# A chunked RWKV-7 recurrence in two groups of four pairs of heads, with a narrower state that VectorE decays

## The chip, the cores and the metric

The kernel runs on one core of a Trainium2 chip. The core has TensorE (PE; its weight loads are shown as PEld), VectorE (DVE), ScalarE (ACT), GpSimd (POOL), SyncE (SP, which issues most DMAs here) and 16 DMA engines. The metric is the device time of one execution of the whole program in microseconds; the median of the runs shown is compared.

## What is computed

A decoder trunk of two layers over 1024 tokens of width 1024 in float32. Layer 0 mixes tokens with a gated MLP, layer 1 with RWKV-7; each is followed by cross-attention into 256 memory rows and a SwiGLU feed-forward. The change lies in RWKV-7's recurrence. It has 16 heads of 64 channels, each with a state of 64 by 64:

```python
def step(S, inp):
    r_t, w_t, k_t, v_t, a_t, b_t = inp
    sa = jnp.einsum('bhij,bhj->bhi', S, a_t)
    S = S * w_t[:, :, None, :] + sa[..., None] * b_t[:, :, None, :] + v_t[..., None] * k_t[:, :, None, :]
    return S, jnp.einsum('bhij,bhj->bhi', S, r_t)
```

Here `a = -kk`, `b = kk * ah`, and `w` is a decay in (0, 1). The output y is normalised by head, gets a bonus term, is multiplied by a gate and projected by `w_o`.

## The kernel before, in words

The 1024 tokens are cut into 16 chunks of 64, and inside a chunk the recurrence is written as matrix products. Four chunks are a batch (256 tokens), so there are four batches, b = 0 to 3. The 16 heads are eight pairs p of two heads (128 channels, which fill the partitions); two pairs that are prepared together are an index pi = 0 to 3.

For each batch the stages are:

- `rwkv_prep(b, pi)` loads the decay's logarithm, keys and so on from DRAM (SP's queue), scans the decay inside each chunk (L1265), takes exponentials, and makes for two pairs: AR (a and r times the decay since the chunk's start), BK (b and k divided by it), the masked products GA and GR of BK with AR (L1300, L1303), BT (BK transposed on TensorE, L1307, copied by ScalarE, L1308), UV (v, and GA times v, L1324) and D, the decay over a whole chunk, one number for each channel (L1272). AR, GR, BT and UV lie in the pool `A`, which has 32 buffers for everything in the kernel; BK and GA take the pool `bk`, which has four.
- `rwkv_solve(b)` inverts the triangular 32 by 32 blocks of GA for all heads and chunks at once: 31 rows in order on VectorE (L1348, L1345) with GpSimd (L1352). Its input and its result go through DRAM (D1 and D4, D2 and D3).
- `rwkv_merge(b)` puts the 32-blocks together into Z, the inverse of the 64 by 64 blocks (32 by 32 products on TensorE, L1386 and L1395).
- `rwkv_chunks(b)` is the recurrence: 4 chunks times 8 pairs, 32 steps.
- `rwkv_post(b, pi)` normalises y, adds the bonus, multiplies by the gate and writes z to DRAM.

A step of the recurrence (`one`) for a chunk and a pair goes from engine to engine. The state `s0` of a pair is a 128 by 128 tile, of which only the two diagonal blocks of 64 by 64 are meaningful in the end; one full product with AR gives both the solve's right side and the old state's share of y (L1422). VectorE adds UV (L1423, into `rs`). Two products with Z give u, one for each head, which ScalarE copies into UV (L1429). Then follow a product of the identity with the state (it puts the old state into PSUM), two products of GR with UV for y, and two of BT with UV which add to the state in PSUM. ScalarE copies y over AR (L1438) and copies the state back, times D (L1441). All of these products but the first go through the helper `mm`, so the profile shows them under L1409, and they are told apart by the tiles that they read. A float32 product with a stationary operand is shown as two instructions.

Each step takes one PSUM bank of the pool `ck`, which has four. `order` sets the order in which the program writes the steps (chunk by chunk, pair by pair), with the parts of neighbouring steps woven together. The functions are generators; `stagger` runs several of them in turn, `run` exhausts one, `later` puts one into a queue of tasks, and `tick` and `drain` advance that queue. The scheduler that places the instructions on each engine takes the order in which they are written as a priority and sets up the semaphores.

In `rwkv` the loop over b = 1 to 3 writes the steps of batch b-1, the solve of b, puts the post stage of b-1 into the queue, and writes prep of b+1 and merge of b. For b = 3 it stops after the steps of batch 2 and the solve. The output projection of the first 512 tokens follows; between its two halves (`between`) come the merge and the steps of batch 3.

Of the kernel before, what the change touches and what calls it, by code (L numbers as in the profile page):

```python
# [12 lines left out]
P = 128  # L13
S = 1024
D = 1024
# [6 lines left out]
class Trunk:  # L22
# [1227 lines left out]
    def rwkv_prep(self, R, B, pi, b, d, C):  # L1250
# [43 lines left out]
        for q in range(2):  # L1294
            qs = slice(q * 4, q * 4 + 4)
            for h in range(2):
# [7 lines left out]
                yield  # L1304
            ps = self.bank()
# [95 lines left out]
    def rwkv_chunks(self, R, B, b, states):  # L1401

        nc = self.nc
        heads = [slice(h * 64, h * 64 + 64) for h in range(2)]
        if b == 0:
            for p in range(KD):
                states[p] = R['st'].tile([P, P], F32, name='s', tag=f's{p}')
                nc.gpsimd.memset(states[p], 0.0)
        mm = lambda o, l, r: nc.tensor.matmul(o, lhsT=l, rhs=r, start=False, stop=True, skip_group_check=True)  # L1409

        def one(c4, p):
            pi, c = (p // 2, p % 2 * 4 + c4)
            T = B['T'][pi]
            AR, UV, BT, GR = (T['AR'], T['UV'], T['BT'], T['GR'])
            zr, to = (heads[pi % 2], heads[c % 2])
            bk = self.bank_ck()
            ar, u, sp = (bk[:, 0:128], bk[0:64, 128:256], bk[:, 256:384])
            s0 = states[p]
            last = b == 3 and c4 == 3
            rs = R['rs'][pi % 2][(p // 4 * 2 + p % 2) % 4]  # L1420
            uvc = UV[0:64, c].rearrange('i h v -> i (h v)')
            nc.tensor.matmul(ar, lhsT=AR[:, c, :, :], rhs=s0, start=True, stop=True)  # L1422
            nc.vector.tensor_add(rs[zr, :], ar[0:64, :], uvc)  # L1423
            if not last and False:
                nc.scalar.activation(s0, s0, AF.Copy, scale=T['D'][:, c:c + 1])
            yield
            for h, hs in enumerate(heads):
                mm(u[:, hs], R['Z'][pi // 2][:, h, c, :], rs[:, hs])
            nc.scalar.copy(uvc, u)  # L1429
# [8 lines left out]
            e = lambda: nc.scalar.copy(AR[to, c - c % 2].rearrange('i a v -> i (a v)'), ar[64:128, :])  # L1438
            e()
            if not last:  # L1440
                nc.scalar.activation(s0, sp, AF.Copy, scale=T['D'][:, c:c + 1])  # L1441
            if not 1:
                e()
        order = sorted(((c4, p) for c4 in range(4) for p in range(KD)), key=lambda x: x[0] * 8 + x[1] + 1 * (x[1] // 2))
        if not 1:
            for c4, p in order:
                for _ in one(c4, p):
                    pass
                yield
            return  # L1450
        live = []
        for c4, p in order:
# [56 lines left out]
    def rwkv(self, W, C, filler, mk_close):  # L1509
# [24 lines left out]
        def prep(b):  # L1534
            return stagger([self.rwkv_prep(R, B[b], pi, b, D_[0], C) for pi in range(4)], 7 if b else 6)

        def chunks(b):
            yield from self.rwkv_chunks(R, B[b], b, states)

        def post(b):  # L1540
# [164 lines left out]
```

## Time and profile before

| | us |
|---|---|
| median of 3 runs | 3295.14 (3293.02 to 3295.4) |
| the profiled execution | 3312.53 |
| its span, first to last instruction | 3310.8 |

The profile is of one execution. Its page gives the busy time of each engine; the other views that are used below are a table by stretches of time (busy time of each engine, the number of instructions, then PEclk, the TensorE clock granted as a share of full speed, the busy share of the DMA engines, and GB/s), a timeline of instructions (start, duration, engine, line, operation, out<-in tiles, shape, count of instructions merged into the row), groups of instructions by line and shape (count, then busy time, mean duration in ns, and the idle time of the engine just before them with what ended it), and the list of waits (who waited for whom: total, times, longest). Matrix products overlap in the pipeline, so their cost is read from the distance between starts and not from their durations. A shape such as `128*64 128x64` is a stationary operand of 128 partitions by 64 columns, and an output of 64 columns.

The mean granted clock of the whole span is 0.956.

### The profile page before, as it was taken

The page shows a single profiled execution, that of the slowest core. Times are in us where ns is not written, and L with a number is a line of the kernel's source. Part 1 is how long each engine was busy: PE and PEld are TensorE (multiplying, and loading weights), DVE is VectorE, ACT ScalarE, POOL GpSimd, SP SyncE. Part 2 cuts the span into 40 slices and gives each one's busy share as a digit, 9 for nine tenths or more (in the row PEclk, how much of TensorE's full clock was granted, in tenths as well). Part 3 has the DMA queues.
Part 4 walks back from the last instruction along what each step waited for, and adds up shares of the span by engine and source line. Part 5 has one row for each costly group of instructions (what it writes and reads, how often), then busy time and mean ns, then how long its engine had stood idle before and what let it go on. Part 6 is the DMA issues. An engine that isn't in the chain of part 4 may idle for free. (4 is left out here: it accounts for less than half of the span.)

```text
span 3310.8 us, 44442 instructions
## 1 busy us (share of the span) xinstructions
PE 3135.4 (95%) x16570; PEld 2545.7 (77%) x16570; DVE 2025.2 (61%) x2876; ACT 1490.8 (45%) x2759; POOL 1058.4 (32%) x800
## 2 busy tenths in 40 slices
PE   8999999899999888999889899999999899999897
PEld 6888888778888666888667787887788688887676
DVE  5463545655444998755766567545545744445998
ACT  5443544533333433766743454445545533334332
POOL 0000011443334654311512244223011533334664
PEclk9999999999999999999999888779999999999998
DMA  5622544332222432744956644335554233323322
GB/s 186 204 77 70 197 147 141 114 96 83 77 77 85 144 102 77 238 136 131 301 173 169 169 121 100 105 92 176 178 163 150 65 96 86 86 77 120 103 96 96
DMA packets 448407, 421.97 MB, mean 127 GB/s; under 512 B 76672, under 2 KB 351264, under 8 KB 448192
## 3 DMA queue, kind: packets, MB, share of 16 engines
q1 hardware_dynamic: 441280, 393.96, 38.8%
q0 software_dynamic: 6912, 25.17, 2.4%
q8 instruction: 131, 2.15, 0.3%
q14 instruction: 84, 0.69, 0.1%
HBM read 314.13 MB, written 104.92 MB: 127 GB/s over the span
## 5 line engine op out<-in xcount | busy, mean ns | idle before, releaser
L438 PE MATMUL ps<-a,wh 128*128 128x512 f32 x2464 | 772.6, 399 | 6.1 <-DVE a L119 4.6
L119 DVE TENSOR_TENSOR wl<-wr,wh 128x1024 fp32r<-128x1024 f32 (+1 forms) x369 | 447.6, 1223 | 349.8 <-ACT wh L118 349.2
L438 PEld LDWEIGHTS ps<-a,wh 128*128 128x128 f32 x2464 | 465.6, 189 | 123.2 <-DVE a L119 7.0
L118 ACT CAST wh<-wr 128x1024 fp32r<-128x1024 f32 (+1 forms) x369 | 323.5, 889 | 522.4 <-PE ps L438 180.1
L438 PE MATMUL ps<-a,wl 128*128 128x512 f32 x1232 | 479.6, 397 | 0.0
L606 PE MATMUL ps<-wh,a 128*128 128x512 f32 x1136 | 380.3, 408 | 48.6 <-DVE a L615 32.6
L148 PE MATMUL ps<-a,wh 128*128 128x512 f32 (+1 forms) x848 | 330.3, 395 | 10.9 <-ACT a L118 5.9
L149 PE MATMUL ps<-a,wh 128*128 128x512 f32 (+1 forms) x848 | 325.7, 386 | 2.2 <-DVE a L119 2.2
L150 PE MATMUL ps<-a,wl 128*128 128x512 f32 (+1 forms) x848 | 325.4, 386 | 1.6 <-DVE wl L119 1.5
L148 PE MATMUL ps<-wh,a 128*128 128x512 f32 x800 | 313.9, 402 | 13.7 <-DVE a L1504 4.8
L149 PE MATMUL ps<-wl,a 128*128 128x512 f32 x800 | 318.5, 398 | 0.6 <-DVE wl L119 0.6
L150 PE MATMUL ps<-wh,a 128*128 128x512 f32 x800 | 316.7, 400 | 0.0
L606 PEld LDWEIGHTS ps<-wh,a 128*128 128x128 f32 x1136 | 218.9, 193 | 120.7 <-DVE a L615 32.5
L438 PEld LDWEIGHTS ps<-a,wl 128*128 128x128 f32 x1232 | 233.2, 189 | 57.6 <-DVE wl L119 0.8
L119 DVE TENSOR_TENSOR wl<-s,wh 128x512 fp32r<-128x512 f32 (+1 forms) x200 | 210.8, 1066 | 76.6 <-ACT wh L118 73.7
L118 ACT CAST wh<-s 128x512 fp32r<-128x512 f32 (+1 forms) x200 | 129.8, 662 | 251.0 <-PE ps L438 91.8
L606 PE MATMUL ps<-wl,a 128*128 128x512 f32 x568 | 228.8, 403 | 0.0
L208 POOL TENSOR_TENSOR sm<-sm,mhalf 128x4 f32<-128x4 f32 (+3 forms) x60 | 67.5, 1127 | 498.1 <-DVE sm L228 422.4
L119 DVE TENSOR_TENSOR a<-a 128x1024 fp32r<-128x1024 f32 (+1 forms) x134 | 208.1, 1567 | 24.3 <-ACT a L118 22.3
L615 DVE TENSOR_TENSOR a<-ps,a 128x512 f32<-128x512 f32 x304 | 194.8, 676 | 13.5 <-PE ps L606 13.4
L148 PEld LDWEIGHTS ps<-a,wh 128*128 128x128 f32 x848 | 163.3, 194 | 43.8 <-ACT a L118 6.8
L148 PEld LDWEIGHTS ps<-wh,a 128*128 128x128 f32 x800 | 151.9, 190 | 51.4 <-DVE a L1504 5.3
(273 smaller groups left out, 5631.7 us busy)
## 6 DMA issues: line engine op xcount, KB each, us to landing
wr<-in_ffn_w_in SPq DMA_DIRECT2D x90, 512.0 KB
scr<-t SPq DMA_DIRECT2D x136, 256.0 KB
scr<-t SPq DMA_DIRECT2D x60, 512.0 KB
a<-scr SPq DMA_DIRECT2D x108, 256.0 KB
wr<-in_rw_w_rkv SPq DMA_DIRECT2D x48, 512.0 KB
t<-scr SPq DMA_DIRECT2D x36, 512.0 KB
ld<-scr SPq DMA_DIRECT2D x72, 256.0 KB
wr<-in_xa_wkv SPq DMA_DIRECT2D x32, 512.0 KB
```

The costliest lines, as they stand in the source:

```text
L118: self.nc.scalar.copy(hi, src)
L119: (engine or self.nc.vector).tensor_sub(lo, src, hi)
L148: nc.tensor.matmul(out, lhsT=ah, rhs=bh, start=start, stop=False)
L149: nc.tensor.matmul(out, lhsT=ah, rhs=bl, start=False, stop=False)
L150: nc.tensor.matmul(out, lhsT=al, rhs=bh, start=False, stop=stop)
L208: self.nc.gpsimd.tensor_tensor(out=r, in0=v, in1=self.mhalf[:, 0:n], op=ALU.pow)
L438: self.nc.tensor.matmul(out, lhsT=a, rhs=b, start=start and k == 0 and (i == 0), stop=k == 3 and i == 2, skip_group_check=True)
L606: nc.tensor.matmul(ps, lhsT=a, rhs=b, start=start and k == 0 and (q == 0), stop=k == K - 1 and q == 2, skip_group_check=True)
L615: nc.vector.tensor_add(o, ps, o)
```

## The change

The eight pairs become two groups of four pairs (pi 0 and 1; pi 2 and 3), and a step now serves one chunk of one pi, that is of two pairs: 16 steps in a batch. The state of a pi is a tile of 128 by 2 by 64: for each of its two pairs the two heads lie one under the other on the partitions, with 64 columns each. The first product is made per head, with 64 partitions of AR and of the state, and each head writes its own PSUM bank, so a step takes two banks of `ck`. The additions, the products with Z, GR and BT stay per head and pair; u of both pairs is copied at once. The product with the identity is gone: VectorE now decays the state and adds the product with BT in one instruction for each pair, reading the state from SBUF and the product from PSUM. Since D multiplied the product with BT too, prep now multiplies BK by D on GpSimd, ahead of the transposes that make BT and behind the products that use BK undecayed.

The order changes as well: the steps of group 0 of batch b-1 are woven with prep of batch b for group 1, and the steps of group 1 with the solve of b, with post of group 0 and with prep of batch b+1 for group 0. The steps of batch 3 are written with both groups in turn, and `between` drains the queue ahead of the merge.

In the diff, of the removed code only what runs is shown (the order was chosen by a constant, `o = 3`).

```diff
@@ rwkv_prep
+            nc.gpsimd.tensor_mul(BK[:, qs], BK[:, qs], T['D'][:, qs].rearrange('p (c a t) -> p c a t', a=1, t=1).broadcast_to([P, 4, 2, 64]))
             ps = self.bank()
             for c in range(4):
                 nc.tensor.transpose(ps[:, c * P:(c + 1) * P], BK[:, q * 4 + c, :, :], self.ident)
@@ rwkv_chunks
-    def rwkv_chunks(self, R, B, b, states):
+    def rwkv_chunks(self, R, B, b, states, group):
...
+        pis = range(2 * group, 2 * group + 2)
         if b == 0:
-            for p in range(KD):
-                states[p] = R['st'].tile([P, P], F32, name='s', tag=f's{p}')
+            for pi in pis:
+                states[pi] = R['st'].tile([P, 2, 64], F32, name='s', tag=f's{pi}')
...
-            nc.tensor.matmul(ar, lhsT=AR[:, c, :, :], rhs=s0, start=True, stop=True)
-            nc.vector.tensor_add(rs[zr, :], ar[0:64, :], uvc)
...
-            for h, hs in enumerate(heads):
-                mm(u[:, hs], R['Z'][pi // 2][:, h, c, :], rs[:, hs])
-            nc.scalar.copy(uvc, u)
-            yield
+            bk = [self.bank_ck() for _ in range(2)]
+            s0 = states[pi]
...
+            for p, c, ps in cs:
+                for h, hs in enumerate(heads):
+                    nc.tensor.matmul(bk[h][:, ps], lhsT=AR[hs, c, :, :], rhs=s0[hs, p, :], start=p == 0, stop=True, skip_group_check=True)
+            v2 = lambda x: x.rearrange('i (p v) -> i p v', p=2)
+            for h in range(2):
+                nc.vector.tensor_add(v2(rs[h][zr, :]), v2(bk[h][0:64, 0:128]), uvc[:, :, h])
+            yield
+            u = bk[1][0:64, 128:384]
+            for h in range(2):
+                for p, c, ps in cs:
+                    o = 128 * h + 64 * p
+                    mm(u[:, o:o + 64], Z[:, h, c, :], rs[h][:, ps])
+            nc.scalar.copy(uvc, u.rearrange('i (h p v) -> i p h v', h=2, p=2))
+            yield
+            for h in range(2):
+                for p, c, ps in cs:
+                    mm(bk[h][64:128, ps], GR[:, h, c, :], UV[:, c, h, :])
             if not last:
-                mm(sp, self.ident, s0)
-            for h, hs in enumerate(heads):
-                mm(ar[64:128, hs], GR[:, h, c, :], UV[:, c, h, :])
-            if not last:
-                for h, hs in enumerate(heads[::-1]):
-                    mm(sp[hs, hs], BT[:, c, hs], UV[:, c, hs.start // 64, :])
-            e = lambda: nc.scalar.copy(AR[to, c - c % 2].rearrange('i a v -> i (a v)'), ar[64:128, :])
-            e()
-            if not last:
-                nc.scalar.activation(s0, sp, AF.Copy, scale=T['D'][:, c:c + 1])
+                for p, c, ps in cs:
+                    for h, hs in enumerate(heads):
+                        mm(bk[0][hs, 128 + p * 64:192 + p * 64], BT[:, c, hs], UV[:, c, h, :])
+                for p, c, ps in cs:
+                    nc.vector.scalar_tensor_tensor(out=s0[:, p, :], in0=s0[:, p, :], scalar=T['D'][:, c:c + 1], in1=bk[0][:, 128 + p * 64:192 + p * 64], op0=ALU.mult, op1=ALU.add)
+            for h in range(2):
+                nc.scalar.copy(of(AR[to])[:, :, c4 - c4 % 2, h], v2(bk[h][64:128, 0:128]))
         live = []
-        for c4, p in order:
-            live.insert(0, one(c4, p))
-            live = [g for g in live if next(g, True) is None]
-            yield
+        for c4 in range(4):
+            for pi in pis:
+                live.append(one(c4, pi))
+                live = [g for g in live if next(g, True) is None]
+                yield
@@ rwkv
         for b in range(1, 4):
             sv = self.rwkv_solve(R, B[b])
-            run(chunks(b - 1), sv)
-            self.later(post(b - 1), 1)
+            run(stagger([chunks(b - 1, 0), prep(b, groups[1]) if b > 1 else iter(())], 0))
+            ahead = prep(b + 1, groups[0]) if b < 3 else iter(())
+            rest = stagger([sv, seq(post(b - 1, groups[0]), ahead)], 0)
             if b == 3:
+                live = chunks(b - 1, 1)
+                for _ in live:
+                    next(rest, None)
+                self.later(rest)
+                self.later(post(b - 1, groups[1]), 1)
                 break
-            run(prep(b + 1), rate=1)
-            run(self.rwkv_merge(R, B[b]))
+            run(stagger([chunks(b - 1, 1), rest], 0))
+            self.later(post(b - 1, groups[1]), 1)
+            run(self.rwkv_merge(R, B[b]))
             self.drain()
...
         def between():
+            self.drain()
             run(self.rwkv_merge(R, B[3]))
-            self.drain()
-            run(chunks(3))
+            run(stagger([chunks(3, g) for g in range(2)], 0))
             self.later(post(3), 1)
```

More of the change, by code (lines that the diff above doesn't have):

```diff
@@ L1409, in rwkv_chunks, with one @@
         mm = lambda o, l, r: nc.tensor.matmul(o, lhsT=l, rhs=r, start=False, stop=True, skip_group_check=True)
-        def one(c4, p):
-            pi, c = (p // 2, p % 2 * 4 + c4)
+        def one(c4, pi):
             T = B['T'][pi]
[L1414 to L1418, printed above, removed]
-            last = b == 3 and c4 == 3
[L1420 to L1425, printed above, removed]
-            yield
-            for h, hs in enumerate(heads):
-                mm(u[:, hs], R['Z'][pi // 2][:, h, c, :], rs[:, hs])
-            nc.scalar.copy(uvc, u)
+            AR, UV, BT, GR, Z = (T['AR'], T['UV'], T['BT'], T['GR'], R['Z'][pi // 2])
+            cs = [(p, p * 4 + c4, slice(p * 64, p * 64 + 64)) for p in range(2)]
+            of = lambda x: x.rearrange('i (p c) h v -> i p c h v', p=2)
+            uvc = of(UV[0:64])[:, :, c4]
+            zr, to = (heads[pi % 2], heads[c4 % 2])
+            bk = [self.bank_ck() for _ in range(2)]
+            s0 = states[pi]
+            last = b == 3 and c4 == 3
+            rs = [R['rs'][pi % 2][pi // 2 * 2 + h] for h in range(2)]
+            for p, c, ps in cs:
[4 more added lines that the diff above has]
+                nc.vector.tensor_add(v2(rs[h][zr, :]), v2(bk[h][0:64, 0:128]), uvc[:, :, h])
+            yield
+            u = bk[1][0:64, 128:384]
[4 more added lines that the diff above has]
+            nc.scalar.copy(uvc, u.rearrange('i (h p v) -> i p h v', h=2, p=2))
@@ L1438, in one @@
-            e = lambda: nc.scalar.copy(AR[to, c - c % 2].rearrange('i a v -> i (a v)'), ar[64:128, :])
-            e()
-            if not last:
[L1441 to L1445, printed above, removed]
-            for c4, p in order:
-                for _ in one(c4, p):
-                    pass
-                yield
-            return
@@ L1532, in stagger, with prep, chunks, post @@
                 yield
[L1534 to L1540, printed above, removed]
-            return stagger([self.rwkv_post(R, B[b], pi, b, D_[0], C) for pi in range(4)], 2 if b == 3 else 1)
+        def prep(b, pis=range(4)):
+            return stagger([self.rwkv_prep(R, B[b], pi, b, D_[0], C) for pi in pis], 7 if b else 6)
+        def chunks(b, group):
+            return self.rwkv_chunks(R, B[b], b, states, group)
+        def post(b, pis=range(4)):
+            return stagger([self.rwkv_post(R, B[b], pi, b, D_[0], C) for pi in pis], 2 if b == 3 else 1)
+        def seq(*gens):
+            for g in gens:
+                yield from g
+        groups = [(0, 1), (2, 3)]
         def run(*gens, rate=1):
```

16 lines of the change are left out of this document (2 added, 14 removed).

## The prediction

> **What bounds the kernel now.** I read the page first (part 1), then a table by stage of the stretch in which the recurrence runs, then TensorE's timeline inside one stage.
>
> ```profile
> span 3310.8 us, 44442 instructions
> PE 3135.4 (95%) x16570; PEld 2545.7 (77%) x16570; DVE 2025.2 (61%) x2876; ACT 1490.8 (45%) x2759; POOL 1058.4 (32%) x800
> ```
>
> TensorE is busy for 95% of the span, so instructions taken off it pay wherever nothing else is late. The stretch that the change touches reaches from the first step of batch 0 (1891 us) to the last of batch 3 (2263 us):
>
> ```profile
> core 0: us, PE busy (x) PEld busy (x) DVE busy (x) ACT busy (x) POOL busy (x), PEclk, DMA share, GB/s
> 1891.00:1942.00 51.00, 50.47 (x647) 42.12 (x645) 38.06 (x139) 33.02 (x109) 23.95 (x35) 1.00 0.31 79
> 1942.00:2003.00 61.00, 61.00 (x600) 53.63 (x601) 38.19 (x80) 27.00 (x62) 19.36 (x17) 0.80 0.53 144
> 2003.00:2047.00 44.00, 42.27 (x401) 33.52 (x399) 35.26 (x131) 24.29 (x82) 22.23 (x34) 0.90 0.19 58
> 2047.00:2119.00 72.00, 66.15 (x601) 57.39 (x602) 31.67 (x70) 20.90 (x41) 17.25 (x15) 0.59 0.59 148
> 2119.00:2164.00 45.00, 43.45 (x468) 35.42 (x466) 33.44 (x126) 28.57 (x92) 20.16 (x33) 0.99 0.26 79
> 2164.00:2195.00 31.00, 31.00 (x184) 25.42 (x182) 21.32 (x37) 17.23 (x40) 15.09 (x11) 1.00 0.40 111
> 2195.00:2206.00 11.00, 9.82 (x259) 9.55 (x258) 4.73 (x7) 5.97 (x13) 1.04 (x1) 0.65 0.58 187
> 2206.00:2263.00 57.00, 57.00 (x472) 46.19 (x472) 11.31 (x38) 25.71 (x90) 7.06 (x7) 0.77 0.14 41
> 1891.00:2263.00 372.00, 361.17 (x3618) 303.25 (x3616) 213.99 (x624) 182.68 (x523) 126.15 (x150) 0.83 0.37 100
> ```
>
> The rows are, in order: steps of batch 0 with the solve of batch 1; post, prep and merge, with the first steps of batch 1; the rest of batch 1's steps; post, prep and merge again; batch 2's steps; half of the output projection; a merge; batch 3's steps alone. TensorE is busy 361 of 372 us and its mean granted clock is 0.83. VectorE comes next with 214. The waits of the stretch point the same way, others wait for TensorE:
>
> ```profile
> DVE rs L1423 <- PE ck L1422: 79.6, 54, 6.8
> ACT ar L1438 <- PE ck L1409: 63.2, 100, 1.6
> ```
>
> **The change part by part.** The time of a step is read as the distance between starts on TensorE, since durations overlap. I call a step's products with AR the first, those with Z the second, and those with GR, BT and the identity the third part. A new step does the work of two old ones (two pairs).
>
> ```profile
> 1904.79 0.49 PE L1409 MATMUL ck<-s,ident 128*128 128x128 f32 x2
> 1905.21 0.39 PE L1409 MATMUL ck<-uv,gr 128*64 128x64 f32 x3
> 1905.38 0.27 PE L1409 MATMUL ck<-uv,bt 128*64 128x64 f32 x1
> 1905.43 0.22 PE L1409 MATMUL ck<-uv,gr 128*64 128x64 f32 x1
> 1905.49 0.28 PE L1409 MATMUL ck<-uv,bt 128*64 128x64 f32 x3
> 1905.70 0.49 PE L1409 MATMUL ck<-s,ident 128*128 128x128 f32 x2
> ...
> 1896.64 1.31 PE L1422 MATMUL ck<-s,ar 128*128 128x128 f32 x8
> 1897.87 0.91 PE L1409 MATMUL ck<-rs,z 128*64 128x64 f32 x12
> 1898.71 0.38 PE L1409 MATMUL ck<-s,ident 128*128 128x128 f32 x1
> ```
>
> *Third part.* From one identity product to the next is 0.91 us; the product with the identity takes 0.42 of it (1904.79 to 1905.21), the eight GR and BT instructions 0.49. Two old steps: 1.82. The new one has 16 GR and BT instructions and no identity: at most 2 x 0.49 = 0.98. The second part's row gives 0.84 / 12 = 0.07 an instruction, so eight GR take 0.56; BT instructions of the two heads write different halves of the partitions, and in the rows above the first BT starts (1905.38) while GR's are still being started (1905.43), again in different halves, so I put the eight BT at half, 0.28. I take 0.85.
>
> *Second part.* 0.07 x 8 = 0.56 before and after.
>
> *First part.* Eight instructions serve four pairs in 1.23 us (1896.64 to 1897.87), 0.62 for two. The new form splits each product by head: eight instructions on 64 partitions instead of four on 128. The nearest rows are prep's:
>
> ```profile
> 1971.13 1.71 PE L1300 MATMUL ps<-ar,bk 64*128 64x128 f32 x16
> 1972.77 0.66 PE L1307 MATMUL ps<-ident,bk 128*128 128x128 f32 x4
> 1973.36 1.16 PE L1300 MATMUL ps<-ar,bk 64*128 64x128 f32 x8
> 1974.44 0.38 PE L1409 MATMUL ck<-s,ident 128*128 128x128 f32 x1
> ```
>
> Eight of one head alone take 1.08; sixteen, eight on each half of the partitions, take 1.64 and not 2.16: the halves overlap where both are queued. The new step alternates heads at every product and gives each its own PSUM bank, so I take 0.70, near the 0.62 of full overlap; the other end is 1.08.
>
> Old: 0.62 + 0.56 + 1.82 = 3.00. New: 0.70 + 0.56 + 0.85 = 2.11, between 2.02 and 2.62. That is 0.89 for each of 64 steps, 57 us, less 3 for the last chunk, which had no identity product: 54 (22 to 60). Part of batch 3 runs at a low clock, where the same distance is larger:
>
> ```profile
> 2211.52 0.80 PE L1409 MATMUL ck<-s,ident 128*128 128x128 f32 x2
> ...
> 2213.08 0.80 PE L1409 MATMUL ck<-s,ident 128*128 128x128 f32 x2
> ```
>
> 1.56 and not 0.91. Some five double steps there save 0.8 more: 4 us. **First term: -58.**
>
> *What the smaller number in flight gives back.* The pool `ck` has four banks; an old step held one, a new step holds two, so two are in flight and not four. Then the chain of a step counts. The other engines' terms:
>
> ```profile
> L1441 ACT ACTIVATE s<-ck,D 128x128 f32<-128x128 f32 x120 | 44.1, 368 | 2.6
> L1423 DVE TENSOR_TENSOR rs<-ck,uv 64x128 f32<-64x128 f32 x124 | 34.5, 281 | 81.2 <-PE ck L1422 79.6
> L1438 ACT COPY ar<-ck 64x128 f32<-64x128 f32 x127 | 33.2, 262 | 64.0 <-PE ck L1409 63.2
> L1429 ACT COPY uv<-ck 64x128 f32<-64x128 f32 x128 | 31.0, 255 | 18.7 <-PE ck L1409 15.4 <-DVE rs L1423 0.8
> L1325 ACT COPY uv<-ps 64x512 f32<-64x512 f32 x18 | 10.4, 578 | 13.3 <-PE ps L1324 12.1 <-POOL bk L1281 1.0 <-issue 0.2
> L1345 DVE TENSOR_TENSOR invZ<-invZ,invP 128x29 f32<-128x29 f32 x6 | 1.2, 200 | 0.0
> L1479 POOL TENSOR_TENSOR a<-a,bo 128x512 f32<-128x512 f32 x16 | 18.6, 1172 | 94.6 <-DMA a<-scr 79.5 <-PE ck L1422 13.0 <-PE ck L1409 1.8
> ```
>
> First part 0.70 and its drain 0.28 (the rows of two above last 0.49, the second start lies half of 0.42 behind the first); two additions 0.56; second part 0.56 and drain 0.22; one copy of 64x256, between 0.255 and 0.578, by length 0.36; third part 0.85 and 0.22; two decays on VectorE, 128x64, not in the trace, between 0.20 and 0.28, taken as 0.25 each: 0.50; some 0.05 at seven handovers. Together 4.6 us for a round of two steps, in which TensorE works 4.2. The idle 0.4 in 32 rounds is 13 us. VectorE's queue adds to it beside a solve:
>
> ```profile
> 1904.00 0.49 PE L1422 MATMUL ck<-s,ar 128*128 128x128 f32 x2
> ...
> 1905.24 0.28 DVE L1423 TENSOR_TENSOR rs<-ck,uv 64x128 f32<-64x128 f32 x1
> ```
>
> The product ended at 1904.49 and the addition began 0.75 later, behind the solve's instructions. A new step crosses VectorE twice, 1.5 a round; the second groups of batches 0 to 2 run beside a solve, 12 rounds, 18 us. Of these 31 us, half the rounds now have prep or post beside them, which can fill TensorE's gaps: 15 remain (0 to 31). Queued behind a waiting decay on VectorE are the solve's rows and prep's masks; the solve is needed only at the merge. **Second term: +15.**
>
> *The moved work.* Half of each prep goes beside the first group of the batch before it, half beside the second, both from the stages with clocks of 0.80 and 0.59. 72 us at 0.59 lose 30 us to the clock; moved into stages at 1.00 the gain lies between 0 and 30. Against it, each merge now has only two posts beside it and waits for its solve through DRAM, and on GpSimd the multiplications of prep and post (1.17 in the row of L1479) now stand between those of the solve: 0 to 15. Prep's loads (SP's queue) come while steps run, where DMA was 0.31 busy or less. I take **-5**.
>
> *The rest.* 120 decays of 0.25 add 30 us to VectorE's 214 of 372; ScalarE loses 44 (L1441). GpSimd gets two multiplications of 128x512 per prep, 16 from here on: 16 x 1.17 = 19 us on its 126 of 372, ahead of the BT transposes. Sixteen more lie before 1891 us, beside the projections. Cover: TensorE's other work of prep; without it 1.2 us each, 19. I take **+3**.
>
> Sum: -58 + 15 - 5 + 3 = **-45**. The profiled execution took 3312.5 us, 17 above the median, so the median of 3295.1 becomes **3250**, and a profiled one 3267.
>
> **Rivals.**
>
> *The chain takes the place of TensorE (slower).* If every round waits 0.75 twice at VectorE, and the heads do not overlap in the first part (2 x 0.38), a round is 4.6 + 1.5 + 0.76 = 6.86 against the 4.66 that the forecast comes to (4.6 and 15 - 13 us over 32 rounds). 32 x 2.2 = 70; -45 + 70 = +25: **3320**. It decides from a round of 4.66 + 45 / 32 = 6.1 us. For it: VectorE has 38 of 51 us in the first stage and gets more. Against: batch 3, with VectorE at 11 of 57, has no solve beside it, nor have the first groups.
>
> *The solve sets the pace (no change).*
>
> ```profile
> 1891.00:1930.00 39.00, 17.05 (x61) 1.00 0.16 45
> 1891.00:1930.00 39.00, 9.45 (x29) 1.00 0.16 45
> ```
>
> Its own work on VectorE (L1348, then L1345) is 26.5 us, and merge b has to wait for it. If this chain alone bounds the first two batches, they gain nothing, VectorE's decays stretch each of three solves by some 8 x 2 x 0.25 = 4 us, and only batch 3 gains, 16 x 0.89 + 4 = 18: -18 + 12 = -6, **3290**. Against: TensorE, not VectorE, was busy throughout.
>
> *The clock.* In the last stage TensorE was busy for all 57 us at 0.77, so a low clock can hold under steps alone. At half clock a step costs 2.11 more; 21 such steps more than now (45 / 2.11) use up the gain, 32 make it +23: **3318**. [...] *The other way:* if the moved prep keeps the clock up, -30 and not -5, and the chain costs 5 less: **3215**.
>
> **How the numbers follow.** Forecast 0.50; chain 0.14; solve 0.14; low clock 0.08; high clock 0.14. Low end: -64 (60 and 4) - 30 + 4 = -90, 3205. High end: the slower rival, 3320. Beyond both lie about 2 in 10. What a measurement here can tell from no change is about 0.2%, 6.6 us. Slower: 0.14 + 0.08, and nothing else of weight: 0.22. Same: most of the solve's 0.14: 0.10. Faster: 0.68.
>
> **What would show it.** Right: no group `s,ident`; the first part as 64*128 64x64 with eight starts within 0.8 us; a third part without an identity of under 1 us; the stretch from 1891 us at some 327 us; batch 3 at 35 to 45 us and not 57. Wrong: rounds over 6 us with idle TensorE before L1423's successor or the decay; a granted clock of the stretch well under 0.83; a merge that waits for its solve with TensorE idle.

## The result, and the profile after

The changed kernel took 3323.38 us (median of 4 runs, 3319.85 to 3327.4) beside 3295.27 us for the kernel before (4 runs, 3293.02 to 3308.74): a ratio of 1.0082, 95% interval 1.0057 to 1.0107. It is **slower by some 27 us**, where 45 us less had been forecast. The profiled execution took 3319.85 us. That of before had been 17 us above its median, so the two profiles differ by 7 us only, and what they show has to be read with that in mind.

The page of the changed kernel, part 1:

```profile
span 3318.1 us, 44372 instructions
PE 3093.6 (93%) x16586; PEld 2523.5 (76%) x16586; DVE 2067.7 (62%) x2996; ACT 1444.1 (44%) x2575; POOL 1094.3 (33%) x828
```

TensorE is busy for 42 us less than before, and the span is 7 us longer. So the work left TensorE, and the time did not. The table by stage of the changed kernel (columns as in the prediction's):

```profile
core 0: us, PE busy (x) PEld busy (x) DVE busy (x) ACT busy (x) POOL busy (x), PEclk, DMA share, GB/s
1893.00:1963.00 70.00, 57.74 (x600) 52.18 (x601) 58.06 (x192) 24.45 (x64) 33.48 (x43) 0.78 0.34 94
1963.00:1992.00 29.00, 23.51 (x390) 20.91 (x390) 16.14 (x34) 11.13 (x23) 10.66 (x9) 0.69 0.47 128
1992.00:2036.00 44.00, 39.91 (x408) 36.22 (x404) 21.30 (x61) 14.12 (x36) 11.42 (x12) 0.74 0.32 91
2036.00:2085.00 49.00, 40.63 (x412) 36.43 (x412) 47.74 (x147) 17.76 (x46) 31.36 (x38) 0.76 0.34 95
2085.00:2112.00 27.00, 15.80 (x332) 14.43 (x331) 14.19 (x42) 9.37 (x19) 9.70 (x11) 0.66 0.64 168
2112.00:2146.00 34.00, 33.41 (x342) 29.56 (x342) 16.12 (x48) 10.37 (x29) 7.86 (x9) 0.77 0.36 100
2146.00:2195.00 49.00, 36.99 (x295) 30.57 (x295) 41.98 (x138) 18.05 (x41) 28.94 (x37) 0.72 0.35 102
...
2220.00:2229.00 9.00, 9.00 (x243) 8.93 (x241) 1.73 (x3) 2.49 (x5) 1.04 (x1) 0.50 0.46 149
2229.00:2266.00 37.00, 34.25 (x463) 31.93 (x459) 15.66 (x58) 15.07 (x48) 4.18 (x4) 0.89 0.15 44
1893.00:2266.00 373.00, 314.03 (x3622) 279.56 (x3622) 250.51 (x752) 135.95 (x336) 144.70 (x166) 0.77 0.36 100
```

The first row, the fourth and the seventh are the stages in which steps run beside a solve (of batches 1, 2 and 3). There VectorE is busy for 58 of 70, 48 of 49 and 42 of 49 us, and TensorE has 12, 8 and 12 us of gaps. Batch 3, alone in the row from 2229, takes 37 us where it took 57 (at a clock of 0.89 and 0.77). The whole stretch takes 373 us as against 372.

Two rows balance it. They begin at 1780 us, where batch 0 and its solve are under way in both kernels, and end with the last step. First before, then after:

```profile
1780.00:2263.80 483.80, 459.29 (x4438) 385.37 (x4439) 278.91 (x798) 222.13 (x597) 160.22 (x210) 0.83 0.42 116
```

```profile
1780.00:2269.30 489.30, 419.47 (x4500) 367.65 (x4499) 318.31 (x923) 176.97 (x414) 191.02 (x233) 0.78 0.41 114
```

Busy time times granted clock is an estimate of the work at full clock: 459.29 x 0.83 = 381 before, 419.47 x 0.78 = 327 after, **54 us less**. The rest of the busy time is lost to the clock: 78 and 92, 14 more. And TensorE's idle time is 24.5 (483.80 - 459.29) and 69.8, **45 more**. -54 + 14 + 45 = +5, the difference of the two rows. From the last step to the end the two agree within 2 us (1047 and 1049). The estimate is good to some 15 or 20 us only: the same products come to 445.99 x 0.89 = 397 in e9 (the kernel before) and 397.81 x 0.87 = 346 in e10 (the change), two runs whose rows stand further down. The difference is much the same there, 51. But the 14 for the clock is not more than this uncertainty; the idle time does not depend on it.

What ended TensorE's waits in these two stretches (total, times, longest) tells where the 45 us are. Before, the rows of the steps:

```profile
PE ck L1409 <- DVE rs L1423: 1.7, 3, 0.9
PE ck L1409 <- ACT uv L1429: 1.0, 2, 0.6
PE ck L1422 <- ACT s L1441: 0.9, 3, 0.4
```

After, the six longest:

```profile
PE ck L1411 <- DVE rs L1429: 20.0, 13, 3.6
PE ps L1308 <- POOL bk L1305: 10.2, 9, 3.1
PE ck L1426 <- DVE s L1446: 8.5, 9, 2.3
PE ps L1495 <- POOL a L1488: 6.9, 1, 6.9
PE ck L1426 <- ACT ar L1448: 5.0, 3, 4.4
PE ck L1411 <- ACT uv L1436: 3.8, 5, 1.8
```

A step's products wait for VectorE's addition (L1429), for its decay (L1446), for the copy of y that frees a bank (L1448) and for u (L1436): 38 us together with a smaller row, where it was 4. The second row is new. The transposes that make BT wait 10 us for GpSimd, which multiplies BK by D just ahead of them (L1305). The 6.9 are one wait for post's multiplication on GpSimd, ahead of the merge of batch 2: there TensorE is idle for 11.2 of the 27 us of the row from 2085, the last row of the solve ends at 2094.9, and the merge begins at 2103.3.

How a stall comes about is seen beside the first solve, in slices of 7 us. Before:

```profile
1897.00:1904.00 7.00, 7.00 (x79) 5.79 (x77) 6.71 (x26) 4.43 (x16) 3.47 (x6) 1.00 0.01 2
1904.00:1911.00 7.00, 7.00 (x76) 5.75 (x76) 6.84 (x27) 4.31 (x15) 4.84 (x7) 1.00 0.07 12
1911.00:1918.00 7.00, 7.00 (x89) 5.87 (x87) 6.78 (x27) 4.47 (x15) 4.65 (x8) 1.00 0.06 10
```

After:

```profile
1914.00:1921.00 7.00, 5.82 (x65) 5.20 (x64) 6.87 (x24) 2.16 (x6) 5.00 (x7) 0.76 0.26 77
1921.00:1928.00 7.00, 2.29 (x13) 1.99 (x14) 6.94 (x21) 1.26 (x3) 4.08 (x5) 0.64 0.46 132
1928.00:1935.00 7.00, 4.96 (x52) 4.56 (x52) 6.94 (x24) 2.62 (x7) 4.55 (x6) 0.74 0.00 1
```

VectorE is as full before (6.71 to 6.84 of 7) as after (6.87 to 6.94). What differs is TensorE: never idle before, and down to 2.29 of 7 after. So a full VectorE alone does not stop the steps. Two things differ in what meets it: two steps are in flight and not four, and a step crosses VectorE twice, with the addition and the decay, and not once. The timeline of the changed kernel shows one such stall:

```profile
1928.73 0.68 PE L1411 MATMUL ck<-uv,bt 128*64 128x64 f32 x5
...
1929.89 0.69 DVE L1477 TENSOR_TENSOR a<-ar,sm 128x512 f32<-128x512 f32 x1
1930.49 0.56 DVE L1349 SCALAR_TENSOR_TENSOR invZ<-invZ,invA 128x19 f32<-128x19 f32 x1
...
1930.97 0.68 DVE L1486 TENSOR_REDUCE sm<-ps 128x8 f32<-128x512 f32 x1
...
1931.57 0.46 DVE L1446 SCALAR_TENSOR_TENSOR s<-s,D,ck 128x64 f32<-128x64 f32 x2
...
1931.98 0.40 PE L1426 MATMUL ck<-s,ar 64*128 64x64 f32 x2 [1.85 <-DVE s L1446]
1932.06 0.26 ACT L1448 COPY ar<-ck 64x128 f32<-64x128 f32 x1 [0.41 <-DVE s L1446]
```

BT's products end at 1929.41. The decays (L1446) begin 2.16 us later, behind post's and the solve's instructions; TensorE has stood idle for 1.85 us when the next first part begins, and the copy of y, which frees the bank, comes later still.

### The profile page after: what moved, and what is told of

Same layout as the page of the kernel before. It is cut to its first block, busy times and chain, and to the rows that moved or that the text cites. A ratio compares the mean times of both kernels' runs of the same rounds, so it can differ in the third digit from the quotient of the medians.

```text
span 3318.1 us, 44372 instructions
## 1 busy us (share of the span) xinstructions
PE 3093.6 (93%) x16586; PEld 2523.5 (76%) x16586; DVE 2067.7 (62%) x2996; ACT 1444.1 (44%) x2575; POOL 1094.3 (33%) x828
```

## The experiments

All times are medians in us, with executions of the kernel before beside each run; the ratio is the one to trust, since single executions of the kernel before lie between 3278 and 3317. (It is not the ratio of the two medians, which for e1 would be 1.0030.) "Idle" and "clock" are TensorE's idle time and granted clock from 1780 us to the last step, from the same view as the two rows above. "Steps" is the part of the idle time that ended before a step's product, and "BK" the part that ended when GpSimd had multiplied BK by D, both added up from the list of waits; a dash stands where there is no such multiplication. The kernel before has 24 us idle, 4 of them before steps.

| run | this | before | ratio (95%) | idle | steps | BK | clock |
|---|---|---|---|---|---|---|---|
| the change | 3323.38 | 3295.27 | 1.0082 (1.0057 to 1.0107) | 70 | 38 | 10 | 0.78 |
| e1 new step, old order | 3308.09 | 3298.18 | 1.0014 (0.9998 to 1.0030) | 59 | 33 | 8 | 0.79 |
| e2 old step, new order | 3313.31 | 3298.18 | 1.0048 (1.0030 to 1.0066) | 36 | 6 | - | 0.87 |
| e3 prep behind the solve | 3329.02 | 3298.18 | 1.0081 (1.0052 to 1.0110) | 73 | 40 | 6 | 0.77 |
| e5 e1 with identity | 3332.27 | 3294.77 | 1.0118 (1.0096 to 1.0140) | 37 | 16 | - | 0.79 |
| e6 e1, four in flight | 3305.20 | 3294.77 | 1.0040 (1.0020 to 1.0061) | 59 | 10 | 21 | 0.78 |
| e7 e5, four in flight | 3306.22 | 3294.77 | 1.0038 (1.0009 to 1.0066) | 18 | 4 | - | 0.81 |
| e8 the change, four in flight | 3303.77 | 3294.77 | 1.0026 (1.0010 to 1.0043) | 71 | 30 | 26 | 0.77 |
| e12 before, two in flight | 3311.10 | 3297.12 | 1.0038 (1.0015 to 1.0061) | 33 | 9 | - | 0.88 |
| e9 before, short solve | 3276.44 | 3297.12 | 0.9949 (0.9923 to 0.9974) | 10 | 2 | - | 0.89 |
| e10 the change, short solve | 3256.13 | 3297.12 | 0.9898 (0.9850 to 0.9946) | 27 | 17 | 3 | 0.87 |
| e15 e2, short solve | 3269.26 | 3293.84 | 0.9927 (0.9898 to 0.9955) | 14 | 2 | - | 0.88 |
| e16 e1, short solve | 3245.28 | 3293.84 | 0.9865 (0.9833 to 0.9898) | 24 | 9 | 5 | 0.86 |
| e13 e8, short solve | 3269.04 | 3293.84 | 0.9931 (0.9907 to 0.9956) | 46 | 16 | 20 | 0.82 |
| e14 solve's additions on GpSimd | 3327.89 | 3293.84 | 1.0112 (1.0083 to 1.0141) | 79 | 32 | 18 | 0.76 |
| e11 new step in batch 3 alone | 3290.69 | 3297.12 | 0.9974 (0.9951 to 0.9997) | 27 | 7 | 0 | 0.88 |
| e17 new step in batches 2 and 3 | 3302.59 | 3300.31 | 1.0010 (0.9989 to 1.0031) | | | | |

### The step and the order apart (e1, e2)

e1 keeps the new step and puts the old order back:

```diff
-            run(stagger([chunks(b - 1, 0), prep(b, groups[1]) if b > 1 else iter(())], 0))
...
-            run(stagger([chunks(b - 1, 1), rest], 0))
+            run(stagger([chunks(b - 1, g) for g in range(2)], 0), sv)
+            self.later(post(b - 1), 1)
...
+            run(prep(b + 1), rate=1)
```

> The changed step, written in the order of the kernel before: both groups of a batch in turn, then the solve, post in the queue, prep of all four pi, merge. If the order is what costs (the changed order puts solve, prep, post and the steps' four instructions on VectorE into one stage, where it was busy 48 of 49 us and the steps waited), rounds of two steps come near the 4.24 us that batch 3 shows alone, at most 6 beside a solve, each batch's steps take 34 to 48 us where before took 45 to 51, and the time is 3255 to 3285, faster than before by 10 to 40. If the step itself is what costs (two in flight, two crossings of VectorE), rounds beside the solve stay over 6 us, and the time is 3310 to 3330.

e2 keeps the changed order and puts the old step back (pairs 4 x group to 4 x group + 3, a state of 128 columns, the product with the identity, no multiplication of BK):

> The step of before (one pair, identity product, ScalarE's decay, one bank), with the steps in two groups of four pairs and everything else in the changed order. If the order costs: slower than before, 3305 to 3340, with VectorE saturated beside the solve although each two pairs give it 0.5 us less. If the changed step costs: 3275 to 3300, no slower than before.

The order alone costs 0.48%, 16 us, as the first of e2's two forecasts had it; the step alone 0.14%, 5 us and not measurably anything, with a time between e1's two forecasts. Together they make up most of the 27. The step by itself gains nothing, though it takes the forecast work away: e1's TensorE is busy for 413 us and not 459. The order, on which the prediction had put a gain of 5, is a loss. The traces show where: from the first row of a solve to its last the solves of batches 1, 2 and 3 take 42, 61 and 44 us in e2 and 45, 60 and 43 in the change, where it was 29, 39 and 28 before and 30, 35 and 29 in e1. Ahead of the merge of batch 2 TensorE then waits 9.5 us in one piece in e2, and 6.9 in the change, for post's multiplication on GpSimd, with the solve's result not yet there. In the kernel before that merge waited 5.8.

### What stands beside the solve (e3, e5)

e3 moves the first half of prep from beside the solve to behind it:

```diff
-            rest = stagger([sv, seq(post(b - 1, groups[0]), ahead)], 0)
+            rest = stagger([sv, post(b - 1, groups[0])], 0)
...
+            run(ahead, rate=1)
```

> The changed kernel, with prep of group 0 written behind the stage of group 1's steps, solve and post (ahead of the merge), and not beside it. If VectorE's crowding beside the solve costs: that stage loses 15 us of VectorE's work, its rounds shorten from 9 to 14 us to 6 or so, and the time is 3295 to 3315. If the step costs, or only the clock: within 5 us of the changed kernel, 3318 to 3328.

3329: no better than the change, and its steps wait 40 us as against 38. Prep's crowding beside the solve is not the cost; this idea fell.

e5 takes e1 and gives the decay back to ScalarE, with the identity on TensorE; with it the multiplication of BK by D goes:

```diff
+                mm(bk[0][:, 128:256], self.ident, s0.rearrange('i p v -> i (p v)'))
...
-                    nc.vector.scalar_tensor_tensor(out=s0[:, p, :], ...)
+                    nc.scalar.activation(s0[:, p, :], bk[0][:, 128 + p * 64:192 + p * 64], AF.Copy, scale=T['D'][:, c:c + 1])
```

> The first experiment's kernel (changed step, order of before) with the identity product and ScalarE's decay put back: one product of the identity with the 128 columns of a pi's state, two ScalarE activations of 128x64 with scale D, no multiplication of BK by D. Still two steps in flight. VectorE gives 30 us less to the steps of the stretch, TensorE works 0.3 to 0.42 us more a step (64 steps: 19 to 27 us). If VectorE's load beside the solve is what eats the gain: 3275 to 3295, faster than the first experiment by 10 or more, with rounds beside the solve nearer 5 us. If the two in flight are what eats it: 3305 to 3330, since the chain of a step gets longer by the identity product and the rounds stay over 6 us.

```profile
1780.00:2274.50 494.50, 457.07 (x4568) 395.36 (x4568) 278.58 (x800) 205.62 (x533) 152.22 (x204) 0.79 0.40 112
```

VectorE is back at 278.58 us, as in the kernel before, and the time rises by another 1%, above both forecasts. This does not clear the decays on VectorE: in e5 the steps wait 16 us and not 33, and TensorE's idle time falls from 59 to 37. But TensorE is busy for 457 us and not 413, more than the 19 to 27 us of the identity product come to at a clock of 0.79 (24 to 34); why it is so much more was not found.

### How many steps are in flight (e6, e7, e8, e12)

e6, e7 and e8 take e1, e5 and the changed kernel, and let each step take one bank of each pool, so that four can be in flight:

```diff
-            bk = [self.bank_ck() for _ in range(2)]
+            bk = [self.bank_ck(), self.bank()]
```

> The first experiment's kernel with one of a step's two banks taken from the pool ps, so that four steps can be in flight; VectorE's work is the same. If the limit of two in flight eats the gain: rounds beside the solve overlap, TensorE is busy again there, and the time is 3255 to 3285. If VectorE's load eats it: within 8 us of the first experiment (3300 to 3316), with VectorE as saturated as there.

> Both at once: identity product and ScalarE's decay, and four steps in flight, in the order of before. If the two causes add: the best of the three, 3255 to 3280. If only the number in flight counts: slower than the sixth kernel by TensorE's 19 to 27 us for the identity. If only VectorE's load counts: the same as the fifth.

> The changed kernel, order and all, with one of a step's two banks taken from ps. If two in flight make the changed order slow: 3280 to 3305, 18 us or more off the changed kernel's 3323. If the order's crowding of VectorE does: 3315 to 3330; prep, which uses ps too, may then lose banks to the steps and it may be slower still.

e12 does the opposite to the kernel before: an old step holds two banks, with no work added.

```diff
             bk = self.bank_ck()
-            ar, u, sp = (bk[:, 0:128], bk[0:64, 128:256], bk[:, 256:384])
+            b2 = None if last else self.bank_ck()
+            ar, u = (bk[:, 0:128], bk[0:64, 128:256])
+            sp = None if last else b2[:, 256:384]
```

> The kernel before, but each old step holds two banks of ck (the state's product with the identity goes into the second), so that two old steps are in flight and not four. Nothing is added to any engine. Theory: the number in flight was what the change paid with; with chains of the same length and half the number the steps beside the solve go from 45 to 51 us a batch to 60 or more, and the time rises by 15 to 45 us. Rival: the number in flight doesn't matter beside a solve, VectorE's queue does: within 8 us of the kernel before.

Four in flight take 0.8% off e5 (e7), 0.56% off the change (e8), and nothing off e1 (e6). What they do to the steps themselves shows in the waits before steps, all four kernels in the order of before (us):

| | decay on VectorE | decay on ScalarE |
|---|---|---|
| two in flight | 33 (e1) | 16 (e5) |
| four in flight | 10 (e6) | 4 (e7) |

The kernel before has 4. So both count, the number in flight and the second crossing of VectorE, and neither alone makes the 33. How much of the right column's gain is the decay is not shown apart: its kernels also have the identity product (TensorE is busy for 457 us in e5, and for 413 in e1) and no multiplication of BK. The times do not add up so, because each remedy has a price of its own: e7 pays with the identity product (TensorE is busy for 458 us, and for 422 in e6), and e6 loses elsewhere what its steps gain. In e6:

```profile
PE ps L1308 <- POOL bk L1305: 20.8, 17, 2.5
PE ck L1387 <- DMA x<-scr: 11.5, 1, 11.5
PE ps L1411 <- DVE rs L1429: 4.6, 8, 1.1
```

The wait for BK on GpSimd goes from 8 to 21 us, and that of the merges for the solve's DMA from 6 to 17 (the second row, and 5.1 for z). In e8 BK's wait goes from 10 to 26 and the steps' only from 38 to 30. Its idle time in the stretch is that of the change, and its profiled execution was its slowest (3310.69 us), so its trace does not show where the 0.56% came from. Why BK is waited for longer with four in flight was not tried by itself; e7, which takes the same banks but has no such multiplication, has no such wait. One thing seen in e6 is that its steps are quicker (batch 2 from the third step's first part to the last step's second, 2146.0 to 2176.6 us, 31 us; in e1 2111.7 to 2177.2, 66), but that the first steps of a batch take their `ps` banks early and wait for the rest of the order (the two first of batch 1 have their right sides at 1977 us and copy u 58 us later), and the prep stages, which use the same banks, get longer (1945 to 2030 and 2066 to 2146 us).

Two in flight add 0.38% to the kernel before (e12): 12 us, by the interval 5 to 20, which tells neither its forecast of 15 to 45 nor the rival's 8 from what came. Its steps wait 9 us and not 4, and in its batch 3, where no solve runs, TensorE is busy for 49.20 of 49.20 us.

### Without the solve's rows (e9, e10, e15, e16, e13)

The kernel before, the changed one, e2, e1 and e8, each with the 31 rows of the solve left out, on VectorE and on GpSimd:

```diff
         for i in range(31):
-            if pend:
-                ...
-            for t in range(i + 1, min(i + 3, 32)):
-                nc.vector.scalar_tensor_tensor(out=Z[:, 0:i + 1, t], ...)
-            n = 29 - i
-            ...
             if i % 8 == 6:
```

> The kernel before, with the 31 rows of the solve left out on VectorE and GpSimd (its loads, its memsets, its copies and its stores stay, so the merge gets identity blocks). It is the base for the run that does the same to the changed kernel. If TensorE's own work and clock set the pace before, and not the solve, its time falls little, by 0 to 15 us (to 3280 to 3295). If the solve set the pace of batches 0 and 1, it falls by more than 30.

> The changed kernel with the same 31 rows left out. Theory: its rounds are long because the two steps in flight queue behind the solve's rows on VectorE at both crossings; without the rows they fall to 4.3 to 5 us in all stages, TensorE's idle time in the stretch falls from 59 to 20 us or less, and the time is 20 to 50 us under the kernel before with the same rows left out. Rival: two in flight are too few beside any other work (prep and post cross the same engines), or the solve never mattered: the changed kernel stays within 10 us of the kernel before with the same rows left out, or above it, with rounds of 6 us and more beside prep.

> The old step in groups of four pairs in the changed order, with the 31 rows of the solve left out. With them the order alone cost 16 us. If that came from the solve standing beside half of the steps, nothing is left of it: within 6 us of the kernel before with the same rows left out (3276). If it came from prep and post standing beside steps, it is still 10 to 20 us above that.

> The new step in the order of before (two in flight), with the 31 rows of the solve left out. With the rows it was 10 us above the kernel before. In this order nothing but the tail of post stands beside the steps once the solve is out, so they should run as in batch 3: a round of 4.3 to 4.8 us, and the time is 35 to 55 us under the kernel before with the same rows left out (3221 to 3241). If the saved time is lost in the prep stages even then, it is 3250 to 3265.

> The changed kernel with four steps in flight (each step takes one bank of each pool) and with the 31 rows of the solve left out. If the number in flight is what is left of the loss, TensorE's idle time in the stretch falls from 27 us to some 10 and the time from 3256 to 3235 to 3245, 35 us and more under the kernel before with the same rows left out (3276). If the rest of the gain went to the clock or to the prep stages, it stays at 3250 to 3262.

The stretch in e9 (before), e10 (the change) and e16 (the new step in the old order):

```profile
1780.00:2236.00 456.00, 445.99 (x4470) 374.06 (x4469) 190.00 (x441) 221.07 (x594) 91.28 (x94) 0.89 0.44 122
```

```profile
1780.00:2205.00 425.00, 397.81 (x4501) 347.03 (x4500) 225.29 (x563) 174.16 (x410) 122.37 (x117) 0.87 0.47 130
```

```profile
1780.00:2196.80 416.80, 392.60 (x4468) 348.09 (x4467) 226.51 (x558) 172.51 (x409) 119.81 (x116) 0.86 0.47 131
```

This tells most. Without the rows the change is **faster**, by 0.51% (1.0 - 0.9898 less 1.0 - 0.9949), 17 us; the new step alone by 0.84%, 28 us; and the order alone by 0.22%, which the intervals do not tell from nothing. The two intervals just reach each other for the change as well, but three of its four executions (3254 to 3256) lie below the lowest of e9's ten (3266); the new step's lie clear. With the rows the same three are +27, +5 and +16. So the rows of the solve cost the kernel before 17 us and the changed one 61 (by the ratios), and the 44 between are what the change pays for meeting them; by the intervals each of these is good to some 8 to 20 us. The same sum gives 40 us for the order alone, 49 for the step alone and 31 for the change with four in flight. In the trace of e10 the steps wait 17 us and not 38, and BK is waited for 3 and not 10. In the trace of e16 the steps run as they were forecast to, here beside nothing:

```profile
2098.26 1.64 PE L1416 MATMUL ck<-s,ar 64*128 64x64 f32 x16
2099.82 1.15 PE L1401 MATMUL ck<-rs,z 128*64 128x64 f32 x16
2100.95 0.50 PE L1401 MATMUL ck<-uv,gr 128*64 128x64 f32 x5
...
2102.50 1.64 PE L1416 MATMUL ck<-s,ar 64*128 64x64 f32 x16
```

A round of two steps is 4.24 us, where it is 6 to 14 beside a solve. Of the expected 35 to 55 us for e16, 28 came: TensorE still idles 24 us and not 10. e10 was expected 20 to 50 us under e9 and is 17 to 20, with rounds of 8 to 10 us beside post and prep and not 4.3 to 5; there prep's products fill TensorE (27 us idle in the whole stretch), as the prediction had it. e13 missed: four in flight bring nothing without the solve (its ratio and e10's can't be told apart). Its steps wait 16 us and e10's 17, so there was little to give back, and the wait for BK goes from 3 to 20.

### VectorE's share or the solve's chain (e14)

```diff
-                (nc.gpsimd if 99 <= i <= 0 else nc.vector).tensor_add(pend[0], pend[0], pend[1])
+                nc.gpsimd.tensor_add(pend[0], pend[0], pend[1])
```

> The changed kernel with the solve's additions (29 for each solve, about 11 us of VectorE) on GpSimd. If the steps wait because VectorE is occupied, the stages with a solve get shorter and the time falls by 10 to 30 us (3295 to 3313). If it is the length of the solve's chain that counts (its rows in order, then DRAM, then the merge), the slower additions make the time rise by 5 to 25 us.

VectorE has 302 us in the stretch and not 318, and the time is no shorter; the ratio is 1.0112, its interval overlaps that of the change. Its trace says why: the rows left on VectorE now wait for GpSimd (15.4 us over the four solves),

```profile
who waited for it (us, times):
  DVE invZ L1349: 15.4, 20
```

and the decays behind them wait as well. One decay had its last product at 2178.65 us; VectorE stood idle from 2178.91 to 2179.96 for GpSimd's addition, did a row of the solve, and began the decay at 2180.56. GpSimd is also later with BK (18 us and not 10). So this run does not separate the two causes: here VectorE's waiting blocks the steps as its work does. What stays open is how much of the 44 us is VectorE's occupation and how much its waiting.

### Versions that keep the gain (e11, e17)

e11 is the kernel before with the new step in batch 3 alone, where no solve runs:

```diff
-            run(chunks(3))
+            run(stagger([self.rwkv_chunks_new(R, B[3], 3, states, g) for g in range(2)], 0))
```

In it, `rwkv_chunks_new` is the changed kernel's `rwkv_chunks`, reads the diagonal blocks of the old states in its first chunk and writes them side by side; only prep of batch 3 multiplies BK by D.

> The kernel before, its step and its order in batches 0 to 2, with the new step in batch 3 alone (prep of batch 3 multiplies BK by D; the first new step of each pair reads the diagonal blocks of the old state and writes them side by side). Theory: where nothing else runs beside the steps the new one is worth what was forecast. Batch 3 took 57 us before and 36 in the changed kernel, so the time falls by 15 to 21 us, to some 3277 (3272 to 3284). Rival: the stage gets shorter but the output projection's second half, which follows, loses as much to its loads or to the clock: 3290 to 3300.

```profile
2187.00:2230.00 43.00, 38.61 (x505) 35.72 (x503) 19.53 (x70) 15.11 (x51) 7.14 (x7) 0.86 0.21 62
```

Its stage takes 43 us as against 57. The time is 0.26% below the kernel before (interval 0.03 to 0.49%), 6 to 9 us, and so below both kernels. This is less than the 14 of the stage. The 57 us of the kernel before were at a clock of 0.77, though, and the 43 at 0.86: the same old steps of batch 3 take 52.4 us at 0.88 in e2, and beside those the new ones are worth 9.

e17 adds batch 2 to it and puts the solve of batch 3 beside the output projection:

```diff
+            elif b == 3:
+                run(stagger([self.rwkv_chunks_new(R, B[2], 2, states, g) for g in range(2)], 0))
+                self.later(sv)
```

> As the kernel with the new step in batch 3 alone, but with the new step in batches 2 and 3, and with the solve of batch 3 put into the queue of tasks, beside the output projection's first half (31 us), instead of beside the steps of batch 2. Theory: the steps of batch 2 run alone in rounds of 4.3 to 5 us, 36 to 40 us where the kernel before had 45, and the projection hides the solve: 5 to 10 us less than with the new step in batch 3 alone (3290), 3280 to 3287. Rival: the solve's rows and its trip through DRAM take longer than the projection's half, the merge of batch 3 waits with TensorE idle, and the time is 3295 to 3320.

3302.59, no different from before: the rival's figure. Its profiled execution took 8306 us, so no stage of it can be read, and whether the merge waited as the rival says is open. One more execution of the kernel before by itself (e4) took 3307.92 us, with a stretch of 484 us as in its first profile. It lay 10 us above the median, so what it was to show of a run near 3295 stays open:

> The kernel before, unchanged, for a second profile. Its first profiled execution took 3312.5 us against a median of 3295. If the time that TensorE spends at half clock differs from run to run, the span and the clock differ together: a run near 3295 shows a mean clock of the stretch 1891 to 2263 above 0.83, and the steps of batch 3 shorter than 57 us. Every theory expects this.

## Why the prediction was wrong

**First term, -58: right.** TensorE's work fell by 54 us at full clock, as estimated above. A step was put at 0.70 + 0.56 + 0.85 = 2.11. In batch 3 of the changed kernel:

```profile
2236.88 1.64 PE L1426 MATMUL ck<-s,ar 64*128 64x64 f32 x16
2238.45 1.15 PE L1411 MATMUL ck<-rs,z 128*64 128x64 f32 x16
2239.59 0.50 PE L1411 MATMUL ck<-uv,gr 128*64 128x64 f32 x5
...
2240.33 0.46 PE L1411 MATMUL ck<-uv,gr 128*64 128x64 f32 x5
...
2241.13 1.64 PE L1426 MATMUL ck<-s,ar 64*128 64x64 f32 x16
```

The two first parts take 1.57 (0.79 a step), the second parts 1.14 (0.57), one third part 0.74, together 2.10. That the sum comes out to 0.01 is luck: the first part is 0.09 longer than put, the third 0.11 shorter. The heads do overlap in the first part, if not wholly. The round is 4.25 (forecast 4.6), the stage some 37 (forecast 35 to 45).

**Second term, +15: this is the step that failed.** It took the idle time of a round from the sum of its parts, added 0.75 for each crossing of VectorE beside a solve, and halved the sum because prep or post would fill TensorE's gaps. The sum was 31 and the half 15; measured, TensorE waits 38 us before steps where it waited 4, with prep and post beside them. The wait of 0.75 had been read from a kernel with four steps in flight, in which TensorE was 7.00 of 7.00 busy beside a VectorE as full as after; it was the wait of one step among four, and harmless. With two in flight both steps stand in VectorE's queue, twice each, and TensorE, ScalarE (9.6 us for the decay beside the first solve) and the banks wait with them: rounds of 6 to 14 us, and 45 us more idle time in all. The runs that show it: the waits before steps are 33 us in e1, 10 with four in flight (e6), 16 with the decay on ScalarE and the identity product (e5) and 4 with both (e7); without the solve's rows those of the change fall from 38 to 17, and the rows cost 17 us before and 61 after. Nor did prep fill the gaps beside a solve: VectorE holds it up too (beside the first one ScalarE waited 3.15 us for prep's D, up to 1923.98, and 3.98 for its scan, up to 1951.02), and so does GpSimd (beside the second one a transpose waited 3.06 us for BK, up to 2088.43; the sum of such waits is below).

**Third term, -5: of the wrong sign.** The order costs 16 us with the solve and nothing measurable without it. The prediction counted post's and prep's multiplications on GpSimd against the solve, but not that eight new steps instead of sixteen, and post and prep with them, meet it on VectorE. The solves take half as long again (43 to 60 us where it was 28 to 39), and the merge behind them waits. Which neighbour stretches them was not separated (e3 moved half of prep away and gained nothing).

**The rest, +3: too small.** The multiplication of BK by D on GpSimd was put at 19 us without cover, 1.2 each, and at next to nothing since prep's other products would cover it. They often did not: TensorE waited for it 6 times in the change from 1891 us on, 5.9 us, and 3 times more between 1780 and 1891, which the sum had left out (10.2 us in all); with four in flight it was 25.6 us in 17 waits (e8). So the 1.2 was about right and the cover was not. The decays are what they were put at: VectorE has 39 us more in the stretch (forecast 30). They cost by where they stand in VectorE's queue, up to half of the waits before steps in e1 (33 against 16 in e5).

**The rivals.** The slower one, the chain in TensorE's place, is what happened, and its 3320 was the time within 4 us. That is partly luck, since its price came out of other numbers: the heads overlap, against its 0.76, and the rounds are not 6.86 everywhere but 4.25 without a solve and far longer beside it. It had been given 0.14 because the argument against it (no solve beside batch 3 and the first groups) was right for half of the rounds and took the other half as bounded by 0.75. The rival of the solve as the pace had the right culprit but not the way in which it works, since the solve did not delay its merge alone. A merge did wait, one of the prediction's own signs of being wrong: 8 us of idle TensorE right ahead of that of batch 2 (6.9 and 1.2). The low clock may be a part of it, 0.78 and not 0.83 in the stretch, but its 14 us are no more than the estimate's uncertainty.

## What to carry to other kernels

A wait that is read from a trace holds for the number of steps that were in flight there; where a change halves that number, each wait at an engine that the steps share (VectorE here, where a decay began 2.16 us after the products that it needed) has to be counted as the whole round's, and the question is what else stands in that queue, not how busy the engine is (6.71 to 6.84 of 7 us before, with TensorE at 7.00 of 7.00, and 6.87 to 6.94 after, with TensorE down to 2.29). A saving on the busiest engine should be tried first in the stage where nothing else runs, and moved only there if the others take it back. Work that goes to an engine with much idle time (GpSimd, 33% busy over the span) still costs if it is put between two products of the busy one (10.2 us of TensorE's waits here). And taking the suspected neighbour out of both kernels (here the solve's rows) tells more than moving it about.

## What the runs showed of the hardware that was not expected

The granted clock did not follow TensorE's busy time as recorded. In the changed kernel it was 0.50 over 2220 to 2229 us with TensorE busy for 9.00 of 9.00 us, and over 1949 to 1956 us:

```profile
1949.00:1956.00 7.00, 6.99 (x54) 6.28 (x52) 6.94 (x18) 3.39 (x7) 1.31 (x1) 0.50 0.79 241
```

What lowers the clock, and what brings it back, is not shown by any run here. Over the whole stretch fewer gaps and a higher clock go together in some pairs (24 us idle at 0.83 before, 10 at 0.89 without the solve's rows) and not in others (18 us idle at 0.81 in e7, 33 at 0.88 in e12).
